# First layer of a two-layer trunk: five weight row blocks loaded on ScalarE's queue and split two per token tile, and the attention outputs split on VectorE alone

## The chip, the cores and the metric

The kernel runs on one core of a Trainium2 chip. The core has a matrix engine (TensorE, PE in the rows, with its weight loads as PEld), VectorE (DVE), ScalarE (ACT), GpSimd (POOL), and SyncE (SP), which here only issues DMA transfers. ScalarE can issue DMA transfers as well; its issues are listed as ACTq, SyncE's as SPq. The metric is the time of one execution in microseconds (us); lower is better.

## What is computed

The input is 1024 tokens of width 1024. Layer 0 normalises them, projects them with one matrix of 3072 columns, and splits the result: columns 0 to 1535 are queries, keys and values of an attention with 8 heads of 64, columns 1536 to 3071 feed a gated short convolution. Both outputs side by side go through one output projection and are added to the input. Layer 1 is a retention layer. Each layer ends in a gated MLP. In short:

```
xn   = rms_norm(x, even_norm)
proj = xn @ w_in                      # (1024 x 1024) @ (1024 x 3072)
q, k, v, gate_b, gate_c, h = split(proj)
a    = dilated_attention(rms_norm(q), rms_norm(k), v)
b    = gate_b * conv3(gate_c * h)
x    = x + concat(a, b) @ w_out
x    = x + conv_glu_ffn(rms_norm(x)) ; then the retention layer and its MLP
```

Everything is float32. A product is made of float32r matmuls: each operand is split into a rounded part (hi) and the rest (lo), and three products hi·hi, hi·lo and lo·hi are summed (`PASSES`).

## The kernel before

**The split.** `split` (L107) makes the hi part with a copy on ScalarE (L109) and the lo part with a subtraction on the engine given, or on GpSimd where none is given (L110). `hilo` splits a loaded weight block `raw` of 128 rows x 512 columns into a tile `hl`. There are 5 `raw` buffers and 7 `hl` buffers.

**The start.** SyncE loads token tile 0 into `xb`, the identity, the two halves of the gain row (`g`), token tile 1, some small rows (`r0`; four of its pieces are issued by ScalarE), tiles 2 and 3, five weight row blocks (columns 512 to 1023 of `w_in`, the keys), and tiles 4 to 7. Each of the 8 token tiles is then normalised and turned: ScalarE squares and sums it (L163), GpSimd makes the inverse root (L152, L153), VectorE scales it into `xn` (L172, two halves), TensorE transposes `xn` in two groups of four (L179) into banks `n`, and `split` writes hi and lo of the transposed tile to `xT` (hi ScalarE, lo VectorE). Beside the first four tiles one weight block each is split, its lo part on GpSimd (L391).

**The first products.** `natural` (L400) takes four token tiles at a time against a weight row block: 8 blocks x 4 banks x 3 passes = 96 matmuls of 128x512 (L407) for one group; six groups follow, keys, queries and values, two groups each. The first group needs only tiles 0 to 3 of `xT`.

**The output projection's first half.** After the attention, `filler` splits the mixer outputs, which lie in `xb`, into tiles of 1024 columns (`gather`, L614): in the order 1, 3, 5, 7, 0, 2, 4, then 6. Odd ones are convolution outputs, even ones attention outputs. The lo parts of 1, 5, 0 and 6 are made by VectorE, those of 3, 7, 2 and 4 by GpSimd. After each split the input tile is loaded again into its `xb` slot. Then `project((1, 3), ...)` runs 16 sums of 6 matmuls in 2 banks `u` (`sweep`, L321); VectorE adds each bank to `xb` (L333), which frees the bank for the sum after next.

**What sets the order.** Each engine runs its instructions in one fixed order; the order follows from the program and the framework that places the instructions. An instruction that waits holds up all behind it on its engine. DMA transfers issued by SyncE and ScalarE use eight completion semaphores in turn (DMAHW0 to DMAHW7 in the rows of the order), so a transfer that takes a semaphore again is issued only when the earlier transfer on it has landed.

Of the kernel before, what the change touches and what calls it, by code (L numbers as in the profile page):

```python
# [13 lines left out]
P = 128  # L14
T = 1024
D = 1024
NT = T // P
KT = D // P
HALF = 512
# [5 lines left out]
RAW = 5  # L25
# [49 lines left out]
def trunk(tc, a):  # L75
    nc = tc.nc
    act, dve, pool, pe, sync = nc.scalar, nc.vector, nc.gpsimd, nc.tensor, nc.sync
# [26 lines left out]
    def f(ap):  # L104
        return ap.bitcast(F32)

    def split(hi, lo, src, eng=None):  # L107

        act.copy(hi, src)  # L109
        (eng or pool).tensor_tensor(lo, src, f(hi), ALU.subtract)  # L110

    cp = Pool("cp")
    wp = Pool("wp")
# [7 lines left out]
    xb = xp.tile([P, NT, D], "xb")  # L121


    def load(src, n=512):
        raw = wp.tile([P, 512], "raw", RAW)
        sync.dma_start(out=raw if n == 512 else raw.rearrange("p (a n) -> p a n", n=n), in_=src)
        return raw

    def hilo(src, into=None, eng=None):
        hl = wp.tile([P, 2, 512], "hl", HL, F32R) if into is None else into  # L130
        split(hl[:, 0, :], hl[:, 1, :], src, eng)
        return hl
# [5 lines left out]
    def row_block(w, r, c0):  # L138

        return load(w[r * P : (r + 1) * P, c0 : c0 + 512])  # L140
# [14 lines left out]
    def row_gains(g, parts):  # L155

        for i, t in enumerate(parts):
            sync.dma_start(out=t, in_=g[0:1, i * HALF : (i + 1) * HALF].to_broadcast([P, HALF]))
        return parts
# [15 lines left out]
    def turn(xn, h, bank):  # L175

        pt = bank()
        for k in range(4):
            pe.transpose(pt[:, k * P : (k + 1) * P], xn[:, (4 * h + k) * P : (4 * h + k + 1) * P], ident)  # L179
        return pt.rearrange("p (k t) -> p k t", k=4)  # L180
# [167 lines left out]
    w_in = a["even_w_in"][0]  # L348

    def load_x(t):  # L350
        sync.dma_start(out=xb[:, t, :], in_=a["x"][0, t * P : (t + 1) * P, :])
# [2 lines left out]
    sync.dma_start(out=ident, in_=a["c_ident"])  # L354
    g0 = row_gains(a["even_norm"][0:1], [np_.tile([P, HALF], f"g{i}") for i in range(2)])
    load_x(1)
    r0 = np_.tile([P, P], "r0")
    sync.dma_start(out=r0[0:12, :], in_=a["even_sconv_w"][0].rearrange("k (j c) -> (k j) c", c=P))
    sync.dma_start(out=r0[12:28, :], in_=a["ret_gn_gain"][0].rearrange("h (j c) -> (h j) c", c=P))
    for i, g in enumerate((a["even_q_gain"], a["even_k_gain"])):  # L360
        for j in range(2):
            act.dma_start(out=r0[28 + i : 29 + i, j * 64 : (j + 1) * 64], in_=g)
    for t in range(2, 4):
        load_x(t)
    raws = [row_block(w_in, k, 512) for k in range(RAW)]
    for t in range(4, NT):
        load_x(t)
    dve.memset(mhalf, -0.5)
    early = []

# [10 lines left out]
    def n_rows(t):  # L381
        xn = np_.tile([P, D], "xn", 2)
        return normed(xb[:, t, :], inverse_rms(xb[:, t, :], xn), g0, xn)

    xn = n_rows(0)
    for t in range(NT):
        pts = [turn(xn, h, n_bank) for h in range(2)]
        if t + 1 < NT:
            xn = n_rows(t + 1)
        if t < 4:  # L390
            early.append(hilo(raws[t] if t < RAW else row_block(w_in, t, 512)))  # L391
        for h in range(2):
            ks, ts = slice(4 * h, 4 * h + 4), slice(t * P, (t + 1) * P)
            split(xT[:, 0, ks, ts], xT[:, 1, ks, ts], pts[h], dve)
# [219 lines left out]
    def gather(js, into, src=None):  # L614
        for j in js:
            if j == 4:
                hl = [mix["mp"].tile([P, T], "u", 5, F32R) for _ in range(2)]
            else:
                t = into.tile([P, 2, T], "h" if j == 6 else f"ab{j}", dt=F32R)
                hl = [t[:, s, :] for s in range(2)]  # L620
            split(*hl, xb[:, j, :] if src is None else src, dve if j in (1, 5, 0, 6) else None)
            mix[j] = hl
            if src is None:
                load_x(j)
# [10 lines left out]
    def filler():  # L635
        for c in range(4):
            while at["heads"] <= c:
                yield
            yield from gated_conv(c)
        while at["values"] < 4 or at["pairs"] < 3:  # L640
            yield
        vp.close()
        xtp.close()
        mix["mp"] = Pool("mp")
        mix["ab"] = Pool("ab")
        gather((1, 3, 5, 7, 0, 2, 4), mix["ab"])
        for js in ((1, 3), (5, 7)):
            for _ in project(js, (1, 3, 5, 7, 0, 2, 4, 6), u_bank):
                yield from (None,) * 4
# [12 lines left out]
    for n, (pr, qb) in enumerate(units):  # L662
        probs = held
        out = st3 if pr == 3 else xb[:, 2 * pr, :]
# [16 lines left out]
    run(steps)  # L681
    mp = mix["mp"]
    gather((6,), mp, st3)
    tp.close()
    ps.close()
# [622 lines left out]
    for h in range(4):  # L1308
        for n, block in enumerate(blocks):
# [3 lines left out]
            name, i = block  # L1313
# [104 lines left out]
```

## Time and profile before

| what | us |
|---|---|
| median of three runs (2721.56, 2725.92, 2728.98) | 2725.92 |
| the profiled execution | 2726.38 |
| its span, first to last instruction | 2724.6 |
| TensorE busy in the span | 2645.2 |
| first projection matmul starts | 15.71 |
| first group of 96 ends, next begins | 48.25 |
| first split of `gather` on VectorE starts | 424.29 |
| sixth bank of the projection is added | 438.69 |

The span is what the trace covers; 1.8 us of the profiled execution lie outside it. A row of a timeline gives the start, the length, the engine, the source line, the operation, the tiles written and read, a count when several in a row are merged, and in brackets how long the engine stood idle before it and what ended that.

### The profile page before, as it was taken

The numbers are of one execution on the slowest core, as the hardware profiler recorded it, in microseconds if no ns is written. First come the engines' busy times: TensorE is split into PE (matmuls) and PEld (weight loads), VectorE is DVE, ScalarE is ACT, GpSimd is POOL, SyncE is SP. The second block draws the span as 40 slices with busy tenths as digits, with TensorE's granted clock in tenths as the row PEclk, the third lists the DMA queues.
The fourth block names the chain that finished last, engine by engine and source line by source line (L and its number), as shares of the span: only waits on it lengthen the run. The fifth ranks groups of instructions, "written<-read, shape, count | busy, mean of one in ns | idle before, by whom it ended". The sixth has DMA issues, their size and how long they took to land. (4 is left out here: it accounts for less than half of the span.)

```text
span 2724.6 us, 34990 instructions
## 1 busy us (share of the span) xinstructions
PE 2645.2 (97%) x12793; PEld 2166.0 (80%) x12793; DVE 1915.8 (70%) x2950; ACT 1189.9 (44%) x2050; POOL 795.9 (29%) x603
## 2 busy tenths in 40 slices
PE   8999999899999999989999999899999999999999
PEld 6877777778888888868888888788877888887887
DVE  4247776687777789697575765466678777777986
ACT  4345543454444444364444434222235444445444
POOL 6721113533333400032222122344454333331000
PEclk9999999999999999999999999899999999999999
DMA  5310012122222274424554546655422222225654
GB/s 171 104 48 28 24 35 79 38 75 89 74 89 74 86 266 154 152 84 160 176 178 151 195 150 219 244 210 186 155 73 60 78 85 72 88 74 187 206 174 154
DMA packets 258785, 336.74 MB, mean 124 GB/s; under 512 B 15121, under 2 KB 182197, under 8 KB 252469
## 3 DMA queue, kind: packets, MB, share of 16 engines
q1 hardware_dynamic: 224428, 246.94, 28.4%
q10 hardware_dynamic: 34184, 87.57, 8.8%
q8 instruction: 100, 1.64, 0.2%
q14 instruction: 73, 0.59, 0.1%
HBM read 257.38 MB, written 77.07 MB: 123 GB/s over the span
## 5 line engine op out<-in xcount | busy, mean ns | idle before, releaser
L110 POOL TENSOR_TENSOR hl<-raw,hl 128x512 fp32r<-128x512 f32 x347 | 580.9, 1688 | 1250.9 <-ACT hl L109 1231.0
L245 PE MATMUL b<-xc,hl 128*128 128x512 f32 (+1 forms) x2652 | 606.2, 388 | 10.7 <-ACT u L305 5.7
L245 PE MATMUL o<-xc,hl 128*128 128x512 f32 (+1 forms) x2568 | 590.7, 389 | 12.9 <-DVE hl L110 3.3
L245 PEld LDWEIGHTS b<-xc,hl 128*128 128x128 f32 x2652 | 485.9, 189 | 125.2 <-ACT u L305 7.0
L245 PEld LDWEIGHTS o<-xc,hl 128*128 128x128 f32 x2568 | 473.4, 190 | 123.6 <-DVE hl L110 4.2
L109 ACT CAST hl<-raw 128x512 fp32r<-128x512 f32 (+1 forms) x440 | 264.9, 609 | 508.7 <-PE o L328 151.7
L110 DVE TENSOR_TENSOR hl<-s,hl 128x512 fp32r<-128x512 f32 x309 | 223.6, 727 | 222.0 <-ACT hl L109 222.0
L972 DVE SCALAR_TENSOR_TENSOR u<-u,cc,u 128x1022 f32<-128x1022 f32 (+1 forms) x176 | 263.4, 1521 | 0.9
L109 ACT CAST hl<-s 128x512 fp32r<-128x512 f32 x309 | 189.7, 619 | 136.8 <-PE b L245 47.2
L458 PE MATMUL u<-xT,hl 128*128 128x512 f32 x576 | 166.1, 410 | 0.0
L328 PE MATMUL o<-hl,y 128*128 128x512 f32 x672 | 163.6, 397 | 0.0
L905 PE MATMUL o<-hl,hl 128*128 128x512 f32 x600 | 146.3, 394 | 5.0 <-DVE hl L110 3.5
L328 PEld LDWEIGHTS o<-hl,y 128*128 128x128 f32 x672 | 125.6, 188 | 29.4 <-POOL y L110 0.2
L905 PEld LDWEIGHTS o<-hl,hl 128*128 128x128 f32 x600 | 111.3, 188 | 34.4 <-DVE hl L110 7.1
L333 DVE TENSOR_TENSOR xb<-xb,o 128x512 f32<-128x512 f32 x160 | 105.0, 680 | 38.0 <-PE o L328 37.9
L458 PEld LDWEIGHTS u<-xT,hl 128*128 128x128 f32 x576 | 99.4, 189 | 20.7 <-issue 5.7
L970 ACT ACTIVATE u<-u,cc 128x1024 f32<-128x1024 f32 x88 | 100.9, 1151 | 31.3 <-DVE u L312 31.3
L109 ACT CAST hl<-h 128x512 fp32r<-128x512 f32 (+1 forms) x124 | 70.0, 581 | 95.0 <-PE o L905 28.2
L1063 PE MATMUL o<-hl,xc 128*128 128x256 f32 x768 | 95.4, 282 | 0.9 <-DVE hl L110 0.8
L1063 PEld LDWEIGHTS o<-hl,xc 128*128 128x128 f32 x768 | 93.8, 188 | 1.8 <-DVE hl L110 1.0
L110 DVE TENSOR_TENSOR hl<-h,hl 128x512 fp32r<-128x512 f32 (+1 forms) x124 | 78.4, 647 | 21.9 <-ACT hl L109 21.7
L152 POOL TENSOR_SCALAR rr<-ss 128x1 f32<-128x1 f32 (+1 forms) x48 | 13.8, 287 | 254.8 <-ACT s L163 235.9
(220 smaller groups left out, 4009.4 us busy)
## 6 DMA issues: line engine op xcount, KB each, us to landing
raw<-in_ffn_w_up SPq DMA_DIRECT2D x176, 256.0 KB, 3.1
raw<-in_ffn_w_down SPq DMA_DIRECT2D x176, 256.0 KB, 3.3
hs<-u ACTq DMA_DIRECT2D x44, 512.0 KB, 2.7
h<-hs SPq DMA_DIRECT2D x44, 512.0 KB, 6.4
raw<-in_even_w_in SPq DMA_DIRECT2D x73, 256.0 KB, 2.8
qscr<-h ACTq DMA_DIRECT2D x16, 1024.0 KB, 4.0
vscr<-u ACTq DMA_DIRECT2D x32, 512.0 KB, 3.8
raw<-in_ret_wo SPq DMA_DIRECT2D x64, 256.0 KB, 3.2
```

The lines of the kernel that those rows point to most:

```text
L109: act.copy(hi, src)
L110: (eng or pool).tensor_tensor(lo, src, f(hi), ALU.subtract)
L152: pool.tensor_scalar(out, ss, 1.0 / n, EPS, ALU.mult, ALU.add)
L245: pe.matmul(u, hl[:, ws, k * P : (k + 1) * P], xc[b][:, xs, k, cols_], start=(first and k == 0 and i == 0), stop=(k == 3 and i == 2), skip ...
L328: pe.matmul(o, lhs[j](ls, t), ws[j][hf][:, w, :], start=(j == 0 and i == 0), stop=(j == n - 1 and i == 2),)
L333: dve.tensor_tensor(xs, xs, o, ALU.add)
L458: pe.matmul(u, hl(ws, k), xT[:, xs, k, hf * 512 : (hf + 1) * 512], start=(k == 0 and i == 0), stop=(k == KT - 1 and i == 2),)
L905: pe.matmul(o, l[:, ls, c * P : (c + 1) * P], r[:, ws, :], start=(start and i == 0), stop=(stop and i == 2), skip_group_check=True,)
L970: act.mul(c, u, wcol(2, jj))
L972: dve.scalar_tensor_tensor(c[:, d:], u[:, :-d], wcol(2 - d, jj), c[:, d:], ALU.mult, ALU.add)
L1063: pe.matmul(u[t // 2][:, c : c + 256], xc[b][:, xs, k, ts], hl[name][k // 2][:, ws, k % 2 * 256 : k % 2 * 256 + 256], start=(first and k = ...
```

## The change

Three things are changed in the first layer. The five first weight row blocks are issued by ScalarE, at the head of its queue, instead of by SyncE after tiles 2 and 3; the small rows `r0` are all issued by SyncE, after the last token tile. The blocks are split two beside each of tiles 0, 1 and 2 and one beside tile 3 (seven instead of four before the products begin), their lo parts in turn on VectorE and GpSimd. And `gather` gives all lo parts to VectorE.

```diff
@@ the start
     load_x(1)
+    raws = []
+
+    def first_row(k):
+        raws.append(wp.tile([P, HALF], "raw", RAW))
+        act.dma_start(out=raws[-1], in_=w_in[k * P : (k + 1) * P, 512:1024])
+
+    for k in range(3):
+        first_row(k)
+    load_x(2)
+    load_x(3)
+    for k in range(3, RAW):
+        first_row(k)
     r0 = np_.tile([P, P], "r0")
+    for t in range(4, NT):
+        load_x(t)
     sync.dma_start(out=r0[0:12, :], in_=a["even_sconv_w"][0].rearrange("k (j c) -> (k j) c", c=P))
     sync.dma_start(out=r0[12:28, :], in_=a["ret_gn_gain"][0].rearrange("h (j c) -> (h j) c", c=P))
     for i, g in enumerate((a["even_q_gain"], a["even_k_gain"])):
         for j in range(2):
-            act.dma_start(out=r0[28 + i : 29 + i, j * 64 : (j + 1) * 64], in_=g)
-    for t in range(2, 4):
-        load_x(t)
-    raws = [row_block(w_in, k, 512) for k in range(RAW)]
-    for t in range(4, NT):
-        load_x(t)
+            sync.dma_start(out=r0[28 + i : 29 + i, j * 64 : (j + 1) * 64], in_=g)
...
-        if t < 4:
-            early.append(hilo(raws[t] if t < RAW else row_block(w_in, t, 512)))
+        for _ in range((2, 2, 2, 1, 0, 0, 0, 0)[t]):
+            k = len(early)
+            early.append(hilo(raws[k] if k < RAW else row_block(w_in, k, 512), None, (dve, pool)[k % 2]))
@@ gather
-            split(*hl, xb[:, j, :] if src is None else src, dve if j in (1, 5, 0, 6) else None)
+            split(*hl, xb[:, j, :] if src is None else src, dve)
```

Lines behind the start have numbers ten higher in the changed kernel (L407 becomes L417); `split` and `sweep` keep theirs.

**The order on ScalarE at the start.** First the kernel before: four small loads, the table load, the sums of squares of tiles 0 and 1 (`xn` written, `xb` read), and the hi parts of tile 0 (`xT`).

```order
1 L362 DMA r_17_90<-in_even_q_gain 1x64 x2
2 L362 DMA r_17_90<-in_even_k_gain 1x64 x2
3 L163 ACT_TABLE_LOAD
4 L163 ACTIVATE xn_117,ss_118<-xb_71 128x1024 [waits DMAHW1_49]
5 L163 ACTIVATE xn_135,ss_136<-xb_71 128x1024 [waits DMAHW0_49]
6 L109 CAST xT_75<-n_125 128x4x128 [waits PE_49]
7 L109 CAST xT_75<-n_130 128x4x128 [waits PE_49]
```

Now the changed kernel; `raw` is a weight block, `hl` its hi part, and DMAHW0 is the semaphore of the first block's own load.

```order
1 L361 DMA raw_90<-in_even_w_in 128x512
2 L361 DMA raw_92<-in_even_w_in 128x512
3 L361 DMA raw_94<-in_even_w_in 128x512
4 L361 DMA raw_98<-in_even_w_in 128x512
5 L361 DMA raw_100<-in_even_w_in 128x512 [waits DMAHW0_49]
6 L163 ACT_TABLE_LOAD
7 L163 ACTIVATE xn_117,ss_118<-xb_71 128x1024 [waits DMAHW1_49]
8 L109 CAST hl_143<-raw_90 128x512
9 L109 CAST hl_146<-raw_92 128x512 [waits DMAHW2_49]
10 L163 ACTIVATE xn_135,ss_136<-xb_71 128x1024 [waits DMAHW1_49]
11 L109 CAST hl_171<-raw_94 128x512 [waits DMAHW4_49]
12 L109 CAST hl_174<-raw_98 128x512 [waits DMAHW6_49]
13 L109 CAST hl_199<-raw_100 128x512 [waits DMAHW0_49]
14 L109 CAST xT_75<-n_125 128x4x128 [waits PE_49]
```

The fifth load, with its wait, now stands ahead of the table load and of tile 0; five hi parts of weights stand ahead of the first hi part of `xT`.

**The order on VectorE at the output projection.** First the kernel before; `ab` are the split outputs, `xb<-xb,u` (L333) is a bank being added, `h` the last output.

```order
605 L110 TENSOR_TENSOR ab_990_4294<-xb_71,ab_990_4294 128x1024
606 L574 TENSOR_TENSOR ph_4267<-s_4262,ph_4267 128x512
607 L574 TENSOR_TENSOR ph_4279<-s_4275,ph_4279 128x384
608 L110 TENSOR_TENSOR ab_992_4302<-xb_71,ab_992_4302 128x1024
609 L333 TENSOR_TENSOR xb_71<-xb_71,u_4343 128x512
610 L110 TENSOR_TENSOR ab_994_4310<-xb_71,ab_994_4310 128x1024
611 L333 TENSOR_TENSOR xb_71<-xb_71,u_4351 128x512
612 L583 TENSOR_TENSOR st_232_1275<-pv_4235,pvt_4363 64x256
613 L333 TENSOR_TENSOR xb_71<-xb_71,u_4366 128x512
614 L110 TENSOR_TENSOR h_4626<-st_232_1275,h_4626 128x1024
615 L333 TENSOR_TENSOR xb_71<-xb_71,u_4374 128x512
```

Now the changed kernel at the same place.

```order
612 L110 TENSOR_TENSOR ab_990_4296<-xb_71,ab_990_4296 128x1024
613 L110 TENSOR_TENSOR ab_991_4300<-xb_71,ab_991_4300 128x1024
614 L110 TENSOR_TENSOR ab_992_4304<-xb_71,ab_992_4304 128x1024
615 L110 TENSOR_TENSOR ab_993_4308<-xb_71,ab_993_4308 128x1024
616 L110 TENSOR_TENSOR ab_994_4312<-xb_71,ab_994_4312 128x1024
617 L110 TENSOR_TENSOR u_4317<-xb_71,u_4316 128x1024
618 L333 TENSOR_TENSOR xb_71<-xb_71,u_4341 128x512
619 L333 TENSOR_TENSOR xb_71<-xb_71,u_4349 128x512
620 L593 TENSOR_TENSOR st_231_1273<-pv_4233,pvt_4361 64x256
621 L110 TENSOR_TENSOR h_4624<-st_231_1273,h_4624 128x1024
622 L333 TENSOR_TENSOR xb_71<-xb_71,u_4364 128x512
```

Before, the first bank is added behind the second split that VectorE makes; now six splits stand ahead of it, and the last output's split stands ahead of the third bank instead of the fourth.

## Rows read from the trace of the kernel before

**Rows 1.** The page, part 1: busy time, share of the span and instructions of each engine.

```profile
PE 2645.2 (97%) x12793; PEld 2166.0 (80%) x12793; DVE 1915.8 (70%) x2950; ACT 1189.9 (44%) x2050; POOL 795.9 (29%) x603
```

**Rows 2.** Busy time of each engine in stretches of the run: the stretch, its length, busy us of PE, PEld, DVE, ACT and POOL (instructions in brackets), the granted TensorE clock as a share of full speed, the busy share of the DMA engines, GB/s.

```profile
15.71:35.61 19.90, 17.69 (x90) 13.61 (x88) 18.50 (x23) 14.99 (x29) 13.68 (x17) 1.00 0.44 159
35.61:160.00 124.39, 124.36 (x535) 100.54 (x534) 22.89 (x37) 41.27 (x69) 89.24 (x80) 1.00 0.36 105
...
423.21:438.69 15.48, 12.02 (x56) 8.57 (x55) 13.01 (x14) 9.53 (x12) 12.55 (x5) 1.00 0.60 203
438.69:475.06 36.37, 36.36 (x156) 28.91 (x154) 17.91 (x26) 4.35 (x7) 7.55 (x7) 1.00 0.15 51
```

**Rows 3.** Timeline of TensorE at the start.

```profile
16.66 1.08 PE L179 MATMUL n<-ident,xn 128*128 128x128 f32 x4 [0.17 <-DVE xn L172]
17.40 3.48 PE L407 MATMUL u<-hl,xT 128*128 128x512 f32 x9
...
34.65 0.63 PE L179 MATMUL n<-ident,xn 128*128 128x128 f32 x4 [1.05 <-DVE xn L172]
...
35.61 12.81 PE L407 MATMUL u<-hl,xT 128*128 128x512 f32 x54
```

**Rows 4.** Timeline of ScalarE at the start, its DMA issues (ACTq) among it.

```profile
0.72 0.79 ACTq L362 DMA_DIRECT2D r<-in_even_q_gain  x2
...
2.13 1.28 ACT L163 ACT_TABLE_LOAD   x1 [2.13 <-issue]
4.14 1.06 ACT L163 ACTIVATE xn<-xb 128x1024 f32<-128x1024 f32 x1 [0.73 <-DMA xb<-in_x]
...
9.46 1.06 ACT L163 ACTIVATE xn<-xb 128x1024 f32<-128x1024 f32 x1 [4.17 <-DMA xb<-in_x]
...
10.52 1.05 ACT L109 CAST xT<-n 128x512 fp32r<-128x512 f32 x2
```

**Rows 5.** SyncE's DMA issues at the start, in order of time; then, from the view of who waited for whom, what SyncE's queue waited for up to 16 us (us in total, times, longest).

```profile
0.72 0.38 SPq L351 DMA_DIRECT2D xb<-in_x  x1
...
2.59 0.43 SPq L351 DMA_DIRECT2D xb<-in_x  x1
...
SPq L358 <- DMA xb<-in_x: 1.1, 1, 1.1
```

**Rows 6.** The instructions that touch `raw` up to 40 us: the time from a load's issue to its landing (us, least, median, most). Below it, in the columns of group 2, the DMA engines in two stretches.

```profile
DMA to landing us min/median/max: 3.2/5.0/6.8
...
1.00:9.00 8.00, 1.12 (x4) 0.72 (x4) 1.50 (x2) 2.43 (x3) 0.75 (x2) 1.00 0.74 242
9.00:16.00 7.00, 4.11 (x17) 3.32 (x17) 4.44 (x6) 5.64 (x11) 2.92 (x6) 1.00 1.03 403
```

**Rows 7.** Timeline of VectorE at the start.

```profile
11.56 1.42 DVE L172 SCALAR_TENSOR_TENSOR xn<-xb,rr,g 128x512 f32<-128x512 f32 x2 [2.60 <-ACT xT L109]
```

**Rows 8.** Timeline of VectorE while the mixer outputs are split.

```profile
424.29 1.22 DVE L110 TENSOR_TENSOR ab<-xb,ab 128x1024 fp32r<-128x1024 f32 x1 [0.39 <-ACT ab L109]
425.43 1.15 DVE L574 TENSOR_TENSOR ph<-s,ph 128x512 fp32r<-128x512 f32 x2
427.04 2.56 DVE L110 TENSOR_TENSOR ab<-xb,ab 128x1024 fp32r<-128x1024 f32 x1 [0.47 <-ACT ab L109]
429.53 0.67 DVE L333 TENSOR_TENSOR xb<-xb,u 128x512 f32<-128x512 f32 x1
430.13 2.82 DVE L110 TENSOR_TENSOR ab<-xb,ab 128x1024 fp32r<-128x1024 f32 x1
...
433.58 0.42 DVE L583 TENSOR_TENSOR st<-pv,pvt 64x256 f32<-64x256 f32 x1
...
435.11 1.23 DVE L110 TENSOR_TENSOR h<-st,h 128x1024 fp32r<-128x1024 f32 x1 [0.40 <-ACT h L109]
...
438.69 0.69 DVE L333 TENSOR_TENSOR xb<-xb,u 128x512 f32<-128x512 f32 x1 [1.15 <-PE u L328]
```

**Rows 9.** The same place: ScalarE, then GpSimd, then TensorE.

```profile
425.01 4.84 ACT L109 CAST ab<-xb 128x1024 fp32r<-128x1024 f32 x5
...
431.09 0.62 ACT L109 CAST hl<-raw 128x512 fp32r<-128x512 f32 x1
...
434.03 1.05 ACT L109 CAST h<-st 128x1024 fp32r<-128x1024 f32 x1 [2.31 <-DVE st L583]
...
426.14 9.05 POOL L110 TENSOR_TENSOR ab<-xb,ab 128x1024 fp32r<-128x1024 f32 x3 [6.05 <-ACT ab L109]
...
438.55 1.30 POOL L110 TENSOR_TENSOR hl<-raw,hl 128x512 fp32r<-128x512 f32 x1
...
428.58 0.96 PE L328 MATMUL u<-hl,ab 128*128 128x512 f32 x3 [1.15 <-POOL ab L110]
...
433.60 3.06 PE L328 MATMUL u<-hl,ab 128*128 128x512 f32 x12 [1.68 <-DVE xb L333]
436.99 3.29 PE L328 MATMUL u<-hl,ab 128*128 128x512 f32 x13 [0.33 <-DVE xb L333]
```

**Rows 10.** Stretches, in the columns of group 2, at two places where the granted clock falls.

```profile
526.00:528.00 2.00, 0.41 (x3) 0.19 (x1) 2.00 (x4) 1.96 (x4) 0.64 (x2) 1.00 0.00 0
...
530.00:532.00 2.00, 2.00 (x12) 2.00 (x12) 1.96 (x4) 2.00 (x5) 2.00 (x2) 0.53 0.04 12
...
1730.00:1743.00 13.00, 8.14 (x27) 6.57 (x28) 8.00 (x14) 2.76 (x5) 4.83 (x8) 0.50 0.48 174
```

## The prediction

> **What bounds the kernel now.** The page's busy times come first: TensorE is busy for 97% of the span [rows 1], so an edit elsewhere counts only where TensorE waits. The table of stretches shows such places at the change's two sites. From 15.71 us, when the first projection matmul starts, to 35.61 TensorE works 17.69 of 19.90 us; in the 124 us behind it, it never stops. Where the mixer outputs are split (423.21 to 438.69) it works 12.02 of 15.48, and then 36.36 of 36.37 [rows 2]. At both places a later start of the dense stretch is paid in full, an earlier one gained in full, and nothing behind can hide it.
>
> At the start, the timeline of TensorE shows the waits: all are for VectorE's scaled rows `xn` (1.05 us before the last tile), none for a split weight; from 35.61 on 54 matmuls run in 12.81 us, 0.237 each, to 48.4 [rows 3]. The nine at 17.40 take 0.387 each, the pace of the lower clock of 1.2 GHz, though the clock column reads 1.00 there [rows 2, 3]; I go by the pace. The rows of `xn` wait for token tiles: tile 1's sum of squares starts at 9.46, after 4.17 us of waiting for its load [rows 4].
>
> At the split, TensorE first waits 1.15 us for GpSimd's lo part of output 3, then 1.68 us for VectorE to add a bank [rows 9]. VectorE's splits of 1024 columns take 1.22 and 1.23 us alone and 2.56 and 2.82 while GpSimd splits beside them [rows 8, 9].
>
> **The change at the start, step by step.** ScalarE gives up four small loads (0.79 us for two [rows 4]) and issues five blocks of 256 KB. Four go out by about 2.2 us. The fifth reuses the semaphore of the first, so it waits until that has landed; SyncE does the same before: its queue waited 1.1 us for the load of tile 0 [rows 5]. Tile 0, issued at 0.72 [rows 5], is there at 4.14 [rows 4]; a weight load lands 3.2 to 6.8 us after its issue [rows 6]. I take tile 0's 3.4 us, since it leaves at the same moment into the same idle engines: 4.2. With 0.33 us for the issue, 1.28 for the table load [rows 4] and the gaps, the squares of tile 0 start at 5.9 instead of 4.14. Two hi parts of weights, 0.62 each [rows 9], are done by 8.4; VectorE's first split stands ahead of the first `xn`, which moves from about 6.3 to about 8.5. All this ends before 9.46, so tile 1 covers it; with a first landing after 6.8 us it would be covered still.
>
> Tile 1's landing is the gate. SyncE can now issue it only when tile 0 has landed, at 4.2 instead of 2.59 [rows 5], but it queues behind the gain rows on SyncE either way. The new cost is sharing: 1.3 MB of weights now move beside it, 3.2 us at the 403 GB/s of a full stretch; the engines were 0.74 busy from 1 to 9 us, so 2.1 us of that fits into idle time [rows 6]. I take the rest, +1.1: tile 1 at 10.6. Bounds: +0 and +3.2.
>
> From there by the lengths before: squares 10.6 to 11.8; three hi parts of weights, 1.7, to 13.5; the hi parts of tile 0, 1.05 [rows 4], to 14.5, where they ended at 11.6. VectorE's `xn` of tile 1 started 2.1 us after its squares [rows 4, 7], so 12.7 to 14.1, and its transposes end at about 15.3. The first projection matmul stands right behind them: 15.3 against 15.71. But tile 2's first four transposes, done by then before, are still owed: 0.6 to 1.1 us [rows 3]. Of the 2.2 us of waiting up to 35.61 [rows 2] I expect about 1.0 to go: seven blocks are split or nearly so by then instead of four, GpSimd's splits no longer stretch the last rows, and 48 matmuls instead of 55 stand behind the last tile's transposes. Sum: -0.4 + 0.8 - 1.0, about **-0.5 us**. Ends: -2.5 (tile 1 not delayed, no waits left), +2.5 (tile 1 at 12.7, no wait gone).
>
> The small rows `r0` move to the end of SyncE's queue, past the token tiles; they are wanted only by a transpose behind tile 7, near 35 us, and cost nothing while they land within 20 us. The first two weight blocks that SyncE still loads for this group follow them, and are wanted after some 60 of the 96 matmuls.
>
> The Trainium skill, "DMA: Bandwidth & Descriptors", section "Issuing engines are not separate DMA queues", says that loads issued from several engines run on the same DMA engines and interleave, so that a second queue saves only the issue time. By that rule nothing would be hidden, tile 1 would come 3.2 us later, and this term would be about +2; the idle share in the rows speaks for less.
>
> **The change at the split.** Before, three of the first seven lo parts and the eighth are VectorE's; now all are. The diff does not tell what follows, the order does: six splits stand in one row ahead of the first bank that VectorE adds, and TensorE has two banks. ScalarE's hi parts, five in 4.84 us from 425.01 [rows 9], run ahead of them. VectorE is free at 426.6 [rows 8]; six splits of 1.2 end at 433.8. GpSimd now has only a weight block here (hi part at 431.09, 1.30 us of splitting [rows 9]), beside the fifth or sixth split. Two of VectorE's splits lost 2.9 us between them to 6 us of GpSimd's, so I add 0.6: 434.4. Then two banks, 0.67 each, 435.7; the last attention output is put together, 0.42, 436.1; its hi part on ScalarE, 1.05 [rows 9], 437.2; its lo part, 1.23, 438.4, and only then the third bank, 439.1. TensorE, which did the third and fourth sums meanwhile, needs two sums of six (1.4 each) until the sixth bank can be added: 442.0 against 438.69 [rows 8]. **+3.3 us.** What it gains, the 1.15 us of waiting for GpSimd, is lost in the wait for the first bank.
>
> Two things are not in it. Waiting from about 429 to 435 may lower the clock: after the 0.41 us of work in 526 to 528 it stood near half for some 3.4 us [rows 10]. Third and fourth sum then take up to 5 us instead of 2.8; 1.3 of the surplus is covered by the wait for the third bank, so 0 to 1.4. I take 0.2. No gain is possible: six splits in a row take 6.9 us at best (1.15 each), which ends the chain at 441.1, **+2.4**; the upper end is 3.3 + 1.4 + 0.7 for a full block by GpSimd, **+5.4**.
>
> That full block is a rule of the Trainium skill: "SBUF — State Buffer", section "Who interferes with whom", has a VectorE instruction with two inputs in SBUF and a GpSimd instruction that reads SBUF exclude each other, the second waiting for the first. By it the 1.30 us would be lost whole, +4.0 instead of +3.3; the stretched rows show both engines slower at once, 2.56 and 2.82 us against 1.22, and I keep 0.6.
>
> **Rivals.** (1) The weights are not hidden: tile 1 at 12.7, the start +2.0; with +3.5 at the split, +5.5, 2731. For it: the queue is full from 9 us on [rows 6]. (2) The blocks land in idle time and TensorE loses its waits: -2.5 at the start, +2.4 at the split, no net change, 2726; for it speaks the 0.74. This is also how it would look if the DMA side of the change did nothing. (3) The clock, on the slower side: it falls in the wait of 429 to 435 and stays low, as from 1730 to 1743, where 13 us went at 0.50 [rows 10]; half of 13 is 6.5, and with +3.5 and the start's 0 the time is +10, 2736. It decides if TensorE has no full work when the clock is due to rise; against it: from 435 on the sums follow nearly without gaps, where at 1730 TensorE worked 8.14 of 13 us. (4) A gain beyond 8 us would need more idle time than both places hold, 2.2 and 3.5 us [rows 2]; only a change in the clock elsewhere could give it.
>
> **How the numbers follow.** -0.5 + 3.3 + 0.2 = +3.0 on the profiled execution's 2726.38 us (span 2724.6 and 1.8 outside) is 2729.4; that execution lies 0.46 above the median of the three runs, so 2729.0. Chances: the forecast 0.56, rival 1 0.18, rival 2 0.16, rival 3 0.07, rival 4 0.03. The runs before spread over 7.4 us, so that 0.3% (8.2 us) is about what a measurement can tell from no change. The terms' bounds reach from about 0 to +8; with some 4 us of scatter the range is 2722 to 2736. Within 0.3%: forecast, rivals 1 and 2, and a part of 3, together 0.91; slower 0.06; faster 0.03.
>
> **What would show it.** Right: the table load behind a wait near 4 us; the first projection matmul between 14.5 and 16.5; six splits of 1.2 us in a row on VectorE, the first bank added 9 to 11 us after the first split starts (before: 5.2), TensorE idle for over 4 us ahead of it; the sixth bank 17 to 19 us after that split (before: 14.4). Wrong: tile 1's squares before 9.5 or after 12.7; the dense stretch reached over 3 us earlier or later than 48.4; a bank added between the splits; a half clock for more than one short stretch behind 430.

## The result, and the profile after

The changed kernel takes 2729.42 us (median of 22 runs, 2726.07 to 2735.27), the kernel before 2725.21 in 22 runs beside them. The ratio is 1.0016 (95% interval 1.0009 to 1.0022), about 4 us slower. The forecast was 2729.0 in 2722 to 2736, within 0.3% of no change. The profiled execution of the changed kernel took 2735.27 us, its slowest; so its times are compared place by place, and not span with span: of the 8.9 us that its span is longer (2733.5 against 2724.6), 4.1 are there at 480 us, behind both places of the change, and the rest comes later.

The page's first part: TensorE's busy time is 3.2 us more than before [rows 1].

```profile
PE 2648.4 (97%) x12793; PEld 2169.8 (79%) x12793; DVE 1918.7 (70%) x2958; ACT 1190.7 (44%) x2050; POOL 779.5 (29%) x595
```

**The start.** ScalarE's timeline first, then SyncE's issues with the one wait that matters, then TensorE's timeline.

```profile
0.71 4.74 ACTq L361 DMA_DIRECT2D raw<-in_even_w_in  x5
5.48 1.28 ACT L163 ACT_TABLE_LOAD   x1 [5.48 <-DMA raw<-in_even_w_in]
6.77 1.06 ACT L163 ACTIVATE xn<-xb 128x1024 f32<-128x1024 f32 x1
...
11.47 1.06 ACT L163 ACTIVATE xn<-xb 128x1024 f32<-128x1024 f32 x1 [2.52 <-DMA xb<-in_x]
```

```profile
4.89 5.70 SPq L351 DMA_DIRECT2D xb<-in_x  x7
...
SPq L351 <- DMA xb<-in_x: 2.4, 1, 2.4
```

```profile
16.82 3.34 PE L417 MATMUL u<-hl,xT 128*128 128x512 f32 x8
...
31.88 0.63 PE L179 MATMUL n<-ident,xn 128*128 128x128 f32 x4 [0.46 <-DVE xn L172]
...
36.45 0.63 PE L179 MATMUL n<-ident,xn 128*128 128x128 f32 x4 [1.05 <-DVE xn L172]
...
37.41 11.18 PE L417 MATMUL u<-hl,xT 128*128 128x512 f32 x47
48.43 3.89 PE L417 MATMUL n<-hl,xT 128*128 128x512 f32 x16
```

ScalarE's table load stands behind the fifth block's issue, which waited until the first had landed. SyncE's queue waits 2.4 us for the load of tile 0, whose semaphore tile 1's load takes again, and issues tile 1 at 4.89 (before: 2.59 [rows 5]). Tile 1's squares start at 11.47 (9.46 [rows 4]), the first projection matmul at 16.82 (15.71). And yet the second group begins at 48.43, 0.18 later than before: 47 matmuls instead of 54 are left for the dense stretch [rows 3].

**The split of the outputs.** VectorE's timeline, then one row each of ScalarE, GpSimd and TensorE, then stretches in the columns of group 2.

```profile
424.34 1.23 DVE L110 TENSOR_TENSOR ab<-xb,ab 128x1024 fp32r<-128x1024 f32 x1 [0.39 <-ACT ab L109]
...
426.55 5.76 DVE L110 TENSOR_TENSOR ab<-xb,ab 128x1024 fp32r<-128x1024 f32 x5
432.22 2.29 DVE L110 TENSOR_TENSOR u<-xb,u 128x1024 fp32r<-128x1024 f32 x1
434.43 1.27 DVE L333 TENSOR_TENSOR xb<-xb,u 128x512 f32<-128x512 f32 x2
435.74 0.42 DVE L593 TENSOR_TENSOR st<-pv,pvt 64x256 f32<-64x256 f32 x1
437.27 1.23 DVE L110 TENSOR_TENSOR h<-st,h 128x1024 fp32r<-128x1024 f32 x1 [1.11 <-ACT h L109]
438.41 0.68 DVE L333 TENSOR_TENSOR xb<-xb,u 128x512 f32<-128x512 f32 x1
440.16 0.69 DVE L333 TENSOR_TENSOR xb<-xb,u 128x512 f32<-128x512 f32 x1 [1.07 <-PE u L328]
...
442.95 0.69 DVE L333 TENSOR_TENSOR xb<-xb,u 128x512 f32<-128x512 f32 x1 [0.71 <-PE u L328]
```

```profile
436.19 1.04 ACT L109 CAST h<-st 128x1024 fp32r<-128x1024 f32 x1 [4.43 <-DVE st L593]
...
431.84 1.59 POOL L110 TENSOR_TENSOR hl<-raw,hl 128x512 fp32r<-128x512 f32 x1 [11.67 <-ACT hl L109]
...
435.16 13.09 PE L328 MATMUL u<-hl,ab 128*128 128x512 f32 x47 [6.52 <-DVE xb L333]
```

```profile
424.34:435.16 10.82, 4.30 (x22) 2.88 (x20) 10.82 (x11) 7.40 (x10) 1.59 (x1) 0.88 0.72 237
432.55:439.38 6.83, 4.22 (x10) 3.36 (x11) 5.40 (x6) 1.04 (x1) 0.88 (x1) 0.50 0.89 331
```

Six splits stand in one row, and TensorE waits 6.52 us for the first bank. In that wait its clock falls to half, and stays there until 439.38, while TensorE works again from 435.16 on. The sixth bank is added 18.61 us after the first split starts, against 14.40 before [rows 8]. This is +4.2 us, as much as the measured difference (2.5 to 6.0 us by its interval).

### The profile page after: what moved, and what is told of

The parts are those of the page before. It is cut to its first block, busy times and chain, and to the rows that moved or that the text cites. A ratio compares the mean times of both kernels' runs of the same rounds, so it can differ in the third digit from the quotient of the medians.

```text
span 2733.5 us, 34983 instructions
## 1 busy us (share of the span) xinstructions
PE 2648.4 (97%) x12793; PEld 2169.8 (79%) x12793; DVE 1918.7 (70%) x2958; ACT 1190.7 (44%) x2050; POOL 779.5 (29%) x595
## 5 line engine op out<-in xcount | busy, mean ns | idle before, releaser
L333 DVE TENSOR_TENSOR xb<-xb,o 128x512 f32<-128x512 f32 x160 | 105.1, 681 | 37.5 <-PE o L328 37.5
```

Of the source, the lines that this page charges most:

```text
L333: dve.tensor_tensor(xs, xs, o, ALU.add)
```

## The experiments

Two tables first, from the timelines of all profiles. Loads_alone, splits_alone, tile1_second and third_on_vector have one execution each, the profiled one (2726.78, 2723.62, 2721.58 and 2724.47 us, with one of the kernel before at 2725.61); single executions of one kernel lie up to 9 us apart, so these four are read by their timelines alone. Times at the start are in us from the span's start; the last column is the start of the second group's first matmul.

| kernel | start | squares of tile 1 | first projection matmul | second group begins |
|---|---|---|---|---|
| before | old | 9.46 | 15.71 | 48.25 |
| split_alone | old | 9.15 | 15.40 | 47.93 |
| adds_between | old | 9.05 | 15.35 | 47.89 |
| wait_filled | old | 9.02 | 15.41 | 48.11 |
| third_on_vector | old | 9.50 | 15.76 | 48.27 |
| changed kernel | new | 11.47 | 16.82 | 48.43 |
| start_alone | new | 10.89 | 16.25 | 47.65 |
| loads_alone | new loads, old splits | 11.01 | 17.68 | 50.24 |
| splits_alone | old loads, new splits | 9.18 | 15.44 | 46.26 |
| splits_and_between | old loads, new splits | 9.19 | 15.45 | 46.56 |
| tile1_second | below | 7.08 | 14.33 | 45.73 |
| tile1_and_between | below | 7.17 | 14.82 | 46.31 |

The same start lies up to 0.8 us apart in two executions, so that a single value is good to some 0.4. At the split, times count from the start of VectorE's first split of an output. The last column is the first matmul of the projection of outputs 0 and 2, which follows the 32 banks of the odd outputs; it tells what is left of a gain or a loss once all splits are done:

| kernel | first bank added | sixth bank added | outputs 0 and 2 begin |
|---|---|---|---|
| before | 5.24 | 14.40 | 51.64 |
| start_alone | 5.24 | 14.40 | 51.50 |
| loads_alone | 5.24 | 14.39 | 51.48 |
| splits_alone | 5.24 | 14.40 | 51.49 |
| tile1_second | 5.24 | 15.58 | 52.67 |
| changed kernel | 10.09 | 18.61 | 55.70 |
| split_alone | 10.09 | 18.46 | 55.54 |
| wait_filled | 9.02 | 15.65 | 52.89 |
| third_on_vector | 4.47 | 13.62 | 50.86 |
| adds_between | 4.48 | 12.23 | 49.65 |
| tile1_and_between | 4.50 | 12.22 | 49.65 |
| splits_and_between | 4.51 | 12.23 | 49.62 |

Tile1_second has the split of the kernel before and yet loses 1.2 us there; the part on tile 1 shows why.

**The two halves of the change, each alone.** `start_alone` is the changed kernel with the old split of the outputs, `split_alone` the kernel before with the new one (the edit below the other way round):

```diff
-            split(*hl, xb[:, j, :] if src is None else src, dve)
+            split(*hl, xb[:, j, :] if src is None else src, dve if j in (1, 5, 0, 6) else None)
```

> The start as in the changed kernel, the split outputs as before. Theory (the row of six splits costs it all, the start nothing): the first group of 96 ends at 48.4 us, 0.1 to 0.2 later than before, the sixth bank is added at 438.8, and the time stands at 1.000 of the kernel before, within 0.0007. Rival (the later first matmul, 16.82 against 15.71, is carried on and the profile of one execution hides it): the group ends at 49.4, and the ratio is 1.0004 or more; then the split would be worth only 3 us.

> All lo parts of the outputs on VectorE, the start as before. Theory: the first bank is added 10.1 us after the first split starts and the sixth 18.6 us after it, as in the changed kernel; +4.1 us, a ratio of 1.0015 (1.0010 to 1.0020), the granted clock at 0.5 for some 7 us behind the wait. Rival (the two parts of the change need each other, the start's order shifting transfers that the split waits for): under +3 us.

Measured: start_alone 0.9995 (0.9986 to 1.0004), split_alone 1.0015 (1.0006 to 1.0024). Both came as the theory had it. The start costs nothing that can be measured (its interval reaches from 3.8 us faster to 1.1 slower), the split 1.0015 x 2724.3 - 2724.3 = 4.1 us (1.6 to 6.5), and by the trace 18.46 - 14.40 = 4.1.

**Where the splits stand.** `adds_between` keeps all lo parts on VectorE, but hands them out one by one between the sums:

```diff
-        gather((1, 3, 5, 7, 0, 2, 4), mix["ab"])
+        rest = [5, 7, 0, 2, 4]
+        gather((1, 3), mix["ab"])
         for js in ((1, 3), (5, 7)):
             for _ in project(js, (1, 3, 5, 7, 0, 2, 4, 6), u_bank):
+                if rest:
+                    gather((rest.pop(0),), mix["ab"])
                 yield from (None,) * 4
```

> The start as before, all lo parts on VectorE, but only outputs 1 and 3 are split ahead of the first sums; 5, 7, 0, 2 and 4 follow one behind each token tile's two sums, so that adds of banks stand between the splits on VectorE. Theory (the place of the splits costs, not the engine that makes them): first bank added about 5 us after the first split, no wait of TensorE over 1 us behind it, sixth bank 11 us after the first split, against 14.4 before and 18.6 in the changed kernel; 3 us faster than before, ratio 0.999 (0.9984 to 0.9994). Rival (VectorE has too much work there, wherever the splits stand): the sixth bank 16 us or later, no faster than before, 1.000 to 1.001.

VectorE in this run, then the two waits of TensorE:

```profile
426.12 2.35 DVE L110 TENSOR_TENSOR ab<-xb,ab 128x1024 fp32r<-128x1024 f32 x2
428.39 1.28 DVE L333 TENSOR_TENSOR xb<-xb,u 128x512 f32<-128x512 f32 x2
...
431.29 0.68 DVE L333 TENSOR_TENSOR xb<-xb,u 128x512 f32<-128x512 f32 x1
431.88 1.91 DVE L110 TENSOR_TENSOR ab<-xb,ab 128x1024 fp32r<-128x1024 f32 x1
433.72 1.27 DVE L333 TENSOR_TENSOR xb<-xb,u 128x512 f32<-128x512 f32 x2
...
436.14 0.69 DVE L333 TENSOR_TENSOR xb<-xb,u 128x512 f32<-128x512 f32 x1
```

```profile
429.12 4.55 PE L328 MATMUL u<-hl,ab 128*128 128x512 f32 x18 [0.90 <-DVE xb L333]
434.45 11.75 PE L328 MATMUL u<-hl,ab 128*128 128x512 f32 x48 [0.77 <-DVE xb L333]
```

The same engine makes the same splits, and the sixth bank comes 6.2 us earlier than in split_alone, 2.2 earlier than before. So with the engine held, the place of the splits decides; the rival falls. (What the old sharing with GpSimd would do at the new places, no run shows.) Later splits still stand between the banks behind the sixth, and when outputs 0 and 2 begin 1.9 us of the gain are left (49.65 against 51.48 to 51.64). The expected gain was 1 us too large: a split still stands ahead of the first add (0.90 us of waiting), and the split at 431.88 was stretched beside GpSimd's weight block (0.77). The time, 0.9994 (0.9986 to 1.0003), is 1.6 us lower, not clear of no change by itself.

**The clock.** `wait_filled` is split_alone with 24 matmuls more, whose sums nothing reads, in TensorE's wait:

```diff
-            for _ in project(js, (1, 3, 5, 7, 0, 2, 4, 6), u_bank):
+            for n, _ in enumerate(project(js, (1, 3, 5, 7, 0, 2, 4, 6), u_bank)):
+                if js[0] == 1 and n == 0:
+                    d = bank5()
+                    for i in range(24):
+                        pe.matmul(d, mix[1][0][:, :P], mix[1][0][:, :512], start=(i == 0), stop=(i == 24 - 1))
```

> As split alone, with 24 more matmuls of 128x512 behind the first two sums, into a bank that nothing reads, so that TensorE works while it waits for the first bank to be added. Theory (of the 4.2 us at the split about 1 is the lower clock behind the idle stretch): the bank is added at the same time, 10.1 us after the first split; the granted clock stays at full speed; third and fourth sum take 2.8 us instead of 5.0, and the sixth bank is added 17.5 us after the first split; +3.1 us on the kernel before, ratio 1.0011. Rival (the slow sums come from contention on VectorE and the banks, not from the clock): sixth bank at 18.6, 1.0015 or more.

One stretch in split_alone, then the same stretch here (columns of group 2; the granted clock is the third number from the end); then timelines of this run: TensorE with most of the added work, VectorE's sixth split with the two banks behind it, and GpSimd beside it; last, the third and the sixth bank in split_alone.

```profile
432.00:438.00 6.00, 3.25 (x8) 2.57 (x9) 4.86 (x5) 1.05 (x1) 1.02 (x1) 0.50 0.97 367
```

```profile
432.00:438.00 6.00, 5.74 (x27) 4.57 (x26) 5.12 (x7) 1.42 (x2) 2.22 (x1) 1.00 0.91 350
```

```profile
428.11 4.95 PE L652 MATMUL s<-ab 128*128 128x512 f32 x21
...
433.73 12.63 PE L328 MATMUL u<-hl,ab 128*128 128x512 f32 x53 [0.26 <-DVE xb L333]
...
431.86 1.22 DVE L110 TENSOR_TENSOR u<-xb,u 128x1024 fp32r<-128x1024 f32 x1
433.00 1.28 DVE L333 TENSOR_TENSOR xb<-xb,u 128x512 f32<-128x512 f32 x2
...
431.10 3.12 POOL L110 TENSOR_TENSOR hl<-raw,hl 128x512 fp32r<-128x512 f32 x1 [11.28 <-ACT hl L109]
```

```profile
438.00 0.68 DVE L333 TENSOR_TENSOR xb<-xb,u 128x512 f32<-128x512 f32 x1
...
442.39 0.69 DVE L333 TENSOR_TENSOR xb<-xb,u 128x512 f32<-128x512 f32 x1 [0.71 <-PE u L328]
```

With TensorE at work the clock stays at full speed, and the slow sums are gone. So it was the clock, not contention. But the sixth bank came 2.81 us earlier than in split_alone, not 1. Three things add up to that. The sixth split took 1.22 us here and 2.29 there (1.07); GpSimd's one block beside it took 3.12 us, against 1.59 there and 1.30 alone. The framework put the last output's split behind the third bank instead of ahead of it. And the clock: at full speed a bank is added 1.7 us after its sum begins, 1.4 for the sum and 0.3 behind it (before: 436.99 and 438.69 [rows 8, 9]; here 433.73 and 435.43). In split_alone the third bank is added by 438.68, and two sums at full speed would have the sixth added 3.1 us later, at 441.8; it was at 442.39, so about 0.6 is the clock's. What is left, 1.1, is the order: here TensorE runs without a wait from the third sum on, and the sixth bank comes 6.6 us after the first; there, without the lower clock, it would come 7.8 after it (441.8 against 434.02). The time was 1.0006 (0.9997 to 1.0015), where 1.0011 was expected.

**Which engine, with the old order.** `third_on_vector` changes one number of the kernel before, `dve if j in (1, 3, 5, 0, 6)`.

> The start as before; of the outputs only the lo part of output 3, for which TensorE waited 1.15 us, goes from GpSimd to VectorE; GpSimd keeps 7, 2 and 4. Theory (what counts is how much stands ahead of the first add on VectorE, and GpSimd beside it stretches each split): the splits of 3 and 5 take about 2.5 us each, the first bank is added 6.5 to 7.5 us after the first split (5.2 before), the sixth 14 to 16 us after it (14.4 before): no gain, within 1.5 us. Rival (the wait for GpSimd was the loss): that 1.15 us is gained whole, sixth bank at 13.2.

First bank at 4.47, sixth at 13.62: 0.8 us better than before, so my expectation of the first add (6.5 to 7.5) was wrong. GpSimd began its first split only at 428.02, behind VectorE's two splits, which therefore took 2.35 us together. From then on the old waits are back. The sixth bank lies between the theory's 14 to 16 and the rival's 13.2, in neither.

**The start, loads and splits apart.** `loads_alone` has the new transfers with the old splits, `splits_alone` the old transfers with the new splits (both with the old split of the outputs). The edit is that of loads_alone against start_alone; in splits_alone it stands the other way round, against the kernel before:

```diff
-        for _ in range((2, 2, 2, 1, 0, 0, 0, 0)[t]):
-            k = len(early)
-            early.append(hilo(raws[k] if k < RAW else row_block(w_in, k, 512), None, (dve, pool)[k % 2]))
+        if t < 4:
+            early.append(hilo(raws[t] if t < RAW else row_block(w_in, t, 512)))
```

> Only the transfers of the start are moved (five blocks on ScalarE's queue, small rows last); one block is split beside each of the first four tiles, its lo part on GpSimd, as before; the outputs are split as before. Theory (tile 1 comes 2.0 us later and costs that, and the seven early splits give it back): squares of tile 1 at 10.9 to 11.5, waits of TensorE between its first projection matmul and the dense stretch 2 us or more, the first group ends at 49.5 to 50.2, against 47.9 to 48.4 in every run so far. Rival (the later tile is made up by VectorE's other work, whatever is split): the group ends at 47.6 to 48.5.

> Only the splits of the start are changed (2, 2, 2, 1 beside tiles 0 to 3, lo parts in turn on VectorE and GpSimd); all transfers as before; the outputs are split as before. Theory (the early splits are worth about 2 us): tile 1's squares at 9.0 to 9.5, the first group ends at 46.0 to 46.6. Rival (the blocks come behind tile 3 on SyncE's queue, so that ScalarE waits for them ahead of the hi parts of the tokens): the group ends at 48 or later, and ScalarE shows waits for a weight block of over 1 us.

TensorE in loads_alone, then in splits_alone:

```profile
17.68 1.63 PE L416 MATMUL u<-hl,xT 128*128 128x512 f32 x3
...
38.24 12.16 PE L416 MATMUL u<-hl,xT 128*128 128x512 f32 x51
50.24 2.03 PE L416 MATMUL n<-hl,xT 128*128 128x512 f32 x8
```

```profile
15.44 0.78 PE L408 MATMUL u<-hl,xT 128*128 128x512 f32 x1
...
35.45 10.97 PE L408 MATMUL u<-hl,xT 128*128 128x512 f32 x46
46.26 5.96 PE L408 MATMUL n<-hl,xT 128*128 128x512 f32 x25
```

Both came as the theory had it, but for loads_alone's end of the group, 0.04 above its range. Against the mean of the five old starts, 48.09, the loads cost 2.15 us, and the splits (46.26 and 46.56) gain 1.7. With both, at 48.04, the loads cost 1.6 and the splits gain 2.2, so the two are not quite a sum; but the difference, 0.5, is about what one execution leaves open. The start's zero is a loss and a gain that cancel.

**Tile 1 first.** `tile1_second` keeps the new splits of the start (not that of the outputs), loads tile 1 right behind tile 0, and leaves three of the five blocks to SyncE:

```diff
     load_x(0)
+    load_x(1)
     sync.dma_start(out=ident, in_=a["c_ident"])
     ...
-    load_x(1)
-    for k in range(3):
+    for k in range(2):
         first_row(k)
     load_x(2)
     load_x(3)
-    for k in range(3, RAW):
-        first_row(k)
+    raws += [row_block(w_in, k, 512) for k in range(2, RAW)]
```

> The changed kernel's splits at the start, but token tile 1 is the second load on SyncE, and only two blocks go by ScalarE, the other three by SyncE behind tile 3; the outputs are split as before. Theory (tile 1's landing is the gate, and what the changed kernel loses there is the place of its load): squares of tile 1 at 6.5 to 8, first projection matmul at 13.5 to 14.5, the first group ends at 46 to 47, over 1 us earlier than in any run so far. Rival (VectorE, busy 93% of the stretch before the dense one, sets the end): first projection matmul earlier, but the group still ends at 47.6 or later.

VectorE's first `xn` in this run; then, in the columns of group 2, TensorE's stretches at the split of the outputs in the kernel before and, at the same place of the program, in this run.

```profile
9.37 3.76 DVE L172 SCALAR_TENSOR_TENSOR xn<-xb,rr,g 128x512 f32<-128x512 f32 x4 [2.63 <-DMA g<-in_even_norm]
```

```profile
426.64:430.64 4.00, 2.55 (x14) 1.80 (x14) 3.60 (x3) 4.00 (x5) 4.00 (x2) 1.00 0.58 203
430.64:436.64 6.00, 4.32 (x18) 2.89 (x16) 5.54 (x6) 2.10 (x4) 6.00 (x3) 1.00 0.90 288
```

```profile
424.00:428.00 4.00, 2.55 (x14) 1.79 (x14) 3.59 (x3) 4.00 (x5) 4.00 (x2) 1.00 0.61 195
428.00:434.00 6.00, 5.25 (x13) 3.65 (x12) 5.31 (x6) 2.09 (x4) 6.00 (x3) 0.51 0.91 289
```

Squares of tile 1 at 7.08, first projection matmul at 14.33, second group at 45.73 (46.31 in tile1_and_between, which has the same start): 1.8 to 2.4 us better than the old start, so the rival falls. But VectorE's first `xn` now waits for the gain rows until 9.37, and splits_alone, with 46.26 and 46.56 in the two runs of its start, comes within some 0.4 us of it without touching a load. So most of the gain belongs to the splits, and the theory, by which tile 1's landing is the gate, is borne out only in small part.

The stretches show a second thing. With the same program and the same work of TensorE in the four us ahead, the clock stayed at full speed in the kernel before and fell to half here, though TensorE's longest wait in those four us was 1.14 us. The sixth bank came 1.18 us later for it (15.58 against 14.40). So the clock can fall at the old split too, in one execution and not in another; of the five profiles with the old split it did so in this one alone.

**Both places mended.** `tile1_and_between` is tile1_second with the loop of adds_between, `splits_and_between` is splits_alone with it.

> The start of the run with token tile 1 as second load (blocks two by ScalarE, three by SyncE, early splits 2, 2, 2, 1), and all lo parts of the outputs on VectorE with the adds between them, as in the run with the adds between. Theory (the two places are far apart and their gains add): the first group ends at 45.4 to 46.2, 2.2 us earlier than before, the sixth bank is added 12.0 to 12.5 us after the first split, against 14.4; together 4.4 us, ratio 0.9984 (0.9978 to 0.9990). Rival (what is gained at the start is lost in a later wait for transfers or the clock, ahead of 424 us): the first split of the outputs starts less than 1 us earlier than before, ratio 0.9990 or more.

> The changed kernel's early splits with all transfers of the start as before, and all lo parts of the outputs on VectorE with the adds between them. Theory: the first group ends at 46.0 to 46.6, the sixth bank is added 12.0 to 12.5 us after the first split; 1.8 + 2.2 = 4.0 us faster than before, ratio 0.9985 (0.9979 to 0.9991), and 8 us faster than the changed kernel, which has the same splits. Rival: as in the run beside it, 0.9990 or more.

Where outputs 0 and 2 begin, in the kernel before, then in splits_and_between:

```profile
475.93 4.43 PE L328 MATMUL o<-hl,ab 128*128 128x512 f32 x18 [0.87 <-DVE xb L333]
```

```profile
472.34 7.92 PE L328 MATMUL o<-hl,ab 128*128 128x512 f32 x33 [0.87 <-DVE xb L333]
```

Both measured 0.9986 (0.9977 to 0.9995) against the kernel before, 3.8 us faster (1.4 to 6.3): 2721.25 and 2720.45 us, where the kernel before had 2724.87. The trace has 1.5 to 1.8 us at the start and 2.2 at the sixth bank, of which 1.9 last: 3.4 to 3.7, and where outputs 0 and 2 begin 3.6 (472.34) and 4.0 (471.91 in tile1_and_between). Expected were 4.4 and 4.0. The gains add, and the rival falls. Both are the fastest kernels of this study; the second does with fewer edits.

## Why the prediction was right, step by step

**The sum.** Forecast +3.0 us, measured about +4.2 to +4.4; the sign and the range hold. The terms: start -0.5 forecast, 0.0 measured (48.04 over two new starts, 48.09 over five old ones); split +3.3 forecast and the clock +0.2, together +4.1 to +4.2 measured. The range's upper end, 2736, is 2 us below its own sum (2726 + 8 + 4); nothing hangs on it.

**The split's chain** held almost to the tenth: the first bank at 434.4 (434.43), the last output put together at 436.1 (436.16), its hi part done at 437.2 (437.23), the third bank done at 439.1 (439.09). Within it two small errors cancel. Splits in a row take 1.15 us each, not 1.2. And the one beside GpSimd lost 1.06 (2.29 against 1.23), where I had added 0.6. The Trainium skill, "SBUF — State Buffer", section "Who interferes with whom", had the second waiting for the first, so that the whole block is lost. The trace of the changed kernel agrees with the skill better than with my 0.6: VectorE lost 1.06 and GpSimd 0.29 (1.59 against 1.30), together 1.35, about one block. Which of the two loses is not settled by that: in wait_filled it was GpSimd, and VectorE lost nothing.

**The term that was mis-sized is the clock.** I took 0.2 out of 0 to 1.4. The drop came as described ("third and fourth sum then take up to 5 us instead of 2.8"): from the start of the third sum to the add of the fourth bank it took 5.00 us, 435.16 to 440.16, where 3.1 would do at full speed (two sums, and the 0.3 until a bank is added). Of the surplus of 1.9 the wait for the third bank covered 1.1; the other 0.8 counts in full (0.6 in split_alone). It moves the sixth bank from 442.2 to 442.95. My own 442.0 had left out the 0.3. The step that failed is the value taken between the bounds: I forecast a wait of some 6 us, and priced the drop in it near the lower end. Wait_filled shows that filling the wait removes it.

**The start** came to the right sum by terms of the wrong size, and that is luck. Tile 1 was forecast for 10.6 and landed for 10.9 and 11.5, inside the bounds; the first projection matmul was forecast for 15.3 and came at 16.3 and 16.8, the second of them outside the 14.5 to 16.5 that I had named as a sign of being right. The waits up to the dense stretch fell as forecast: idle time of TensorE between the first projection matmul and the second group is 1.52 us in both new starts and 1.81 to 2.76 in the five old ones (2.33 on the mean), 0.8 less where I had said 1.0. The +0.8 for tile 2's owed transposes does not show: TensorE's busy time in that stretch is 29.9 and 30.1 us, against 29.8 to 30.9 in the old starts. So the first matmul comes 1.0 later on the mean, the way from it to the second group is 1.06 shorter, and the two cancel; my terms were -0.4, +0.8 and -1.0.

The step that failed is the issue of tile 1. I counted its later issue as nothing ("it queues behind the gain rows on SyncE either way") and put the cost down to sharing, +1.1. The traces have it the other way round. With the new loads tile 1 is issued at 4.89, 5.05 and 4.90 us, 2.3 to 2.5 later than before; tile 0, with weights beside it, freed the semaphore 0.7 us later than the 4.2 that I had forecast. From its issue tile 1 then took 6.6, 5.8 and 6.1 us (old starts: 6.4 to 6.9), so that the way was not longer with the weights beside it. What I had not seen either is how large the two parts are when apart, 2.2 and 1.7 us.

**The rivals.** Rival 1 (the weights are not hidden, +2.0 at the start) is half right: loads_alone lost 2.15 us, about the size that it gave, though not by its cause. The Trainium skill, "DMA: Bandwidth & Descriptors", section "Issuing engines are not separate DMA queues", said that only issue time is saved. Loads_alone agrees: there is no gain from the second queue. But its tile 1 came 1.8 us later than in the old starts (11.01 against 9.24 on the mean), not the 3.2 of rival 1, and the issue alone was 2.3 later. The splits paid for it, which rival 1 left out. Rival 2 (a wash) falls with split_alone and start_alone: the split costs 4.1 us and the start gives nothing back. Rival 3 (the clock stays low for 13 us) falls: the stretch at 0.50 lasted 6.83 us, and the sums ran without a gap behind 435.16. Rival 4 did not come up.

**What stays open.** Whether tile 1, issued as late, would have landed sooner without the weights ahead of it: no run has the late issue without them (tile1_second removes both). And why the clock falls at the old split in one execution and not in the others.

## What to carry to other kernels

Giving work to a faster engine moves it in that engine's queue too: count what now stands ahead of the instruction that frees the matrix engine's banks, and hand long work out between those instructions. A change that measures as nothing can be a gain and a loss of the same size; run the parts alone, and keep the one that pays. A wait of TensorE costs more than its length when the clock falls in it; here another 0.6 to 0.8 us on 6.5. A difference of 1 us at such a place can also be the clock of one execution (tile1_second), so read the granted clock before the cause.

## What the runs showed that was not expected

- A VectorE split of 1024 columns (1.15 to 1.23 us alone) took 2.29, 2.29 and 1.91 us beside one weight block of GpSimd's, but 1.22 in wait_filled, where GpSimd's block took 3.12 instead of 1.30. One of the two pays for most of the overlap, and not always the same.
- The two executions of the new start differ by 0.6 us in the landing of tile 1 (11.47 and 10.89) and by 0.8 in the end of the group. A start of some 50 us can't be tuned to tenths from one profile.
